# Two small tiles made larger in a hybrid encoder block, so that the matmul operands after them start elsewhere

## The chip, the cores and the metric

The kernel runs on one core of a Trainium2 chip. The metric is the device time of one execution in microseconds (us). "Engines" are TensorE (PE; its weight loads are shown apart as PEld), VectorE (DVE), ScalarE (ACT), GpSimd (POOL) and SyncE (SP), which here issues the DMAs.

## The reference

One encoder layer on 1024 rows of width 1024, in float32:

```python
n = rms_norm(h, attn_norm_w)
aq, ak, av, rq, rk, rv, rg = split(n @ w_in)          # 1024 x 2816
y_attn = windowed_gqa_sink(rope(rms_norm(aq)), rope(rms_norm(ak)), av, sink)
y_ret  = silu(rg) * rms_norm(bidirectional_retention(rope(rq), rope(rk) / 8, rv, log_fwd, log_bwd))
h = h + concat(y_attn, y_ret) @ w_out                 # 1024 x 1024
m = rms_norm(h, ffn_norm_w)
h = h + (silu(m @ w_gate) * (m @ w_up)) @ w_down      # width 2816
```

## The kernel before

Every large operand is split into two float32r tiles, a high part and the rest (`X_hi`/`X_lo`, `wh`/`wl`), and each product is three matmuls: high by high, high by rest, rest by high (`passes`, line 236; `sip`, line 241). A matmul of 128x128 stationary values by a 512-column moving operand writes one PSUM bank. Each matmul has its own weight load, which TensorE runs beside the matmul before it. In rows of the trace, `out<-moving,stationary` is the order of the names.

The work has three stretches. **The front** (to about 526 us) makes the projections: weights come in as tiles of 512 columns and are the *moving* operand, slices of `X_hi`/`X_lo` are stationary (outputs `a`, `b`, `c`, `d`, `o`; `c` in halves of 256 columns). Between these matmuls stand those of retention and attention, which use tiles of the pool `up`; `fill(n)` puts in 3n projection matmuls at given points of the code. **Gate and up** (to about 961 us; `gate_up`, line 986) goes over 22 units, each with seven products of 12 matmuls (a Strassen-like scheme): four with `X_hi`/`X_lo` as the moving operand (the first into `pa`, one into `pb`, two into `pc`), three with `T2`, `T3`, `T4` (all into `pa`); here the weight tile is stationary. **Down** (to about 1171 us; `down`, line 1056) is seven products of 11 x 12 matmuls (`da`, `db`, `dc`), both operands from the weight tiles (`eA..`, `eS..`, tags `wh` and `wl`).

The order of the instructions is set by priorities in the program, and semaphores by what reads and writes which tile. Where a tile stands in a partition of SBUF is set by the pools: one after the other in the order of the code (`const`, `wp`, then `fc`, `up`, `st` of the front; after the front the pools `p2` and `pd` take their place), each tile rounded up to a multiple of 32 bytes. A partition is a run of bytes, and "place" below is the start of an operand in it, as the rest by division by 128. All slices of a tile that matmuls read lie whole multiples of 128 bytes behind its start.

Of the kernel before, what the change touches and what calls it, by code (L numbers as in the profile page):

```python
# [9 lines left out]
F32 = mybir.dt.float32  # L10
F32R = mybir.dt.float32r
AF = mybir.ActivationFunctionType
# [4 lines left out]
P = 128  # L17
# [43 lines left out]
def hymba_block(ctx, tc, x, xT, cst, prm, retw, ffnw, wqkv, wkv, wout, wg, wu, wd, out):  # L61
# [3 lines left out]
    nc = tc.nc  # L65
# [31 lines left out]
    pe, act, dve, pool = (Engine(e) for e in (nc.tensor, nc.scalar, nc.vector, nc.gpsimd))  # L97
# [24 lines left out]
    const = ctx.enter_context(tc.tile_pool(name="const", bufs=1))  # L122
# [4 lines left out]
    fc = front.enter_context(tc.tile_pool(name="fc", bufs=1))  # L127
# [33 lines left out]
    mask = fc.tile([P, 3 * P], F32, name="mask")  # L161
    idx = const.tile([P, 4], F32, name="idx")
    anw = const.tile([P, 8], F32, name="anw")
    prmt = fc.tile([P, 280], F32, name="prmt")
    retw_dm = const.tile([P, DM], F32, name="retw_dm", tag="c4")
    retw_t = retw_dm[:, 0:512]
    mhalf = const.tile([P, 8], F32, name="mhalf")
# [6 lines left out]
    ze = const.tile([P, 2, 8], F32, name="ze")  # L174
    gall = const.tile([P, 2, 8], F32, name="gall")
    gt = const.tile([P, 2, 4], F32, name="gt")

    X_hi = const.tile([P, 8, S], F32R, name="X_hi")
    X_lo = const.tile([P, 8, S], F32R, name="X_lo")
# [132 lines left out]
    def row_rms(t):  # L312
        i = xcount[0] % 8
        xcount[0] += 2
        xv = xs[:, i:i + 2, :]
        nc.sync.dma_start(xv, x[t * P:(t + 1) * P, :].rearrange("p (a c) -> p a c", a=2))
        c = slice(t, t + 1)
        act.activation(xv, xv, AF.Square, accum_out=ssq[:, c])
        dve.tensor_scalar(ssq[:, c], ssq[:, c], 1.0 / DM, EPS, op0=ALU.mult, op1=ALU.add)
        pool.tensor_tensor(rstd[:, c], ssq[:, c], mhalf[:, 0:1], op=ALU.pow)  # L320
        dve.tensor_scalar(rstd8[:, c], rstd[:, c], HD ** -0.5, None, op0=ALU.mult)
        dve.scalar_tensor_tensor(r2[:, c], rstd[:, c], 1.0 / HD, rstd[:, c], op0=ALU.mult, op1=ALU.mult)

    pool.memset(mhalf[:], -0.5)
    warm = const.tile([P, 1], F32, name="warm")

    hold[0] = pinned[0] = True
    act.activation(warm[:], mhalf[:, 0:1], AF.Exp)

    zero = U("zero", "kr", F32R)  # L330
    pool.memset(f32(zero[:]), 0.0)
# [4 lines left out]
    hold[0] = pinned[0] = False  # L336
    for t in range(RMS_AHEAD):
        row_rms(t)
    nc.sync.dma_start(prmt[:], prm)
    nc.sync.dma_start(idx[:], cst[:, 1792:1796])  # L340
    nc.sync.dma_start(cosT[:].rearrange("p t d -> p (t d)"), cst[:, 0:512])
    nc.sync.dma_start(sinT[:].rearrange("p t d -> p (t d)"), cst[:, 512:1024])
# [831 lines left out]
```

## Time and profile before

| | us |
|---|---|
| median of 3 runs | 1179.77 (1178.02 to 1179.95) |
| the profiled execution | 1178.03, span 1176.3 |
| PE busy | 1139.5 (97%) |
| DVE busy | 834.6 (71%) |
| ACT busy | 547.6 (47%) |

A matmul's duration in the trace (about 0.39 us for 512 columns) contains its way through the array, which overlaps the next matmul. What a matmul costs in a full stream is the distance from its start to the next one's start. The chain of waits gives it directly: a piece of n matmuls and its us.

The matmuls of the program before, by width of the moving operand and by place of both operands:

| moving columns | place of moving | place of stationary | matmuls | which |
|---|---|---|---|---|
| 512 | 32 | 0 | 1344 | projections |
| 512 | 0 | 32 | 1056 | gate and up, with X |
| 512 | 32 | 32 | 792 + 924 | gate and up with T; down |
| 512 | 0 | 0 | 100 | attention, and 12 at the start (`idle`) |
| 256 | 32 | 0 | 192 | projection `c` |
| 256, 384 | 0 | 0 | 416 | retention, attention |
| 128 | 0 | 0 or 32 | 560 | transposes, retention |

### The profile page before, as it was taken

What the parts mean: (1) busy time and instruction counts of PE and PEld (TensorE: products, weight loads), DVE (VectorE), ACT (ScalarE), POOL (GpSimd) and SP (SyncE); (2) the same over time, 40 slices, a digit from 0 to 9 for tenths busy, and PEclk for the clock granted to TensorE, in tenths of its full rate; (3) what the DMA queues carried; (4) which work ended last, traced back from release to release, by engine and by line L of the source; (5) the groups of instructions that cost most, each with busy time, mean ns of one, the idle gap of its engine ahead of it and who ended that gap; (6) DMA issues with size and microseconds to landing.
All of it is one profiled execution on the core that took longest, in us unless ns stands there. A gap on an engine that the chain in (4) does not pass through costs nothing.

```text
span 1176.3 us, 16106 instructions
## 1 busy us (share of the span) xinstructions
PE 1139.5 (97%) x5384; PEld 926.9 (79%) x5384; DVE 834.6 (71%) x1632; ACT 547.6 (47%) x1134; POOL 248.5 (21%) x308
## 2 busy tenths in 40 slices
PE   8989998998999999999999999999999999999998
PEld 6767776787878887877888888888888888888887
DVE  6988876888889993689766676567657755555553
ACT  4745534445488863456333333333333335444441
POOL 3445734367545631322000000000000000000000
PEclk9999999999999999999999999999999999999999
DMA  8520112003100023621643554355435668676672
GB/s 290 194 72 1 39 34 70 3 1 91 37 1 2 18 73 112 210 90 63 198 135 124 179 183 138 118 179 187 143 112 177 216 208 290 215 241 192 217 264 72
DMA packets 82594, 152.59 MB, mean 130 GB/s; under 512 B 9424, under 2 KB 9936, under 8 KB 82512
## 3 DMA queue, kind: packets, MB, share of 16 engines
q1 hardware_dynamic: 82512, 151.57, 39.7%
q8 instruction: 42, 0.69, 0.3%
q14 instruction: 40, 0.33, 0.1%
HBM read 111.43 MB, written 40.11 MB: 129 GB/s over the span
## 4 chain that ended last, share of the span: by engine, by line
PE 54%; DVE 3%; issue 2%; POOL 0%; ACT 0%; ACTq 0%; DVEq 0%; POOLq 0%
PE pa L88 21%; PE pc L88 11%; PE da L88 10%; PE dc L88 5%; PE pb L88 5%; PE db L88 3%; DVE h L88 1%; DVE X_lo L88 0%; DVE T L88 0%; DVE xr L88 0%; POOL hr L88 0%; DVE t L88 0%; DVE stash L88 0%; DVE hr L88 0%; DVE S_00l L88 0%
## 5 line engine op out<-in xcount | busy, mean ns | idle before, releaser
L91 POOL TENSOR_TENSOR wl<-raw,wh 128x512 fp32r<-128x512 f32 x44 | 60.2, 1391 | 61.5 <-ACT wh L91 61.0
L88 PE MATMUL a<-wh,X_lo 128*128 128x512 f32 x128 | 51.8, 405 | 1.5 <-DVE X_lo L88 1.4
L88 PE MATMUL a<-wh,X_hi 128*128 128x512 f32 x128 | 51.2, 400 | 1.4 <-DVE krv L88 1.4
L88 PE MATMUL b<-wh,X_hi 128*128 128x512 f32 x128 | 52.4, 409 | 0.0
L88 PE MATMUL o<-wh,X_hi 128*128 128x512 f32 x128 | 51.8, 405 | 0.0
L88 PE MATMUL b<-wh,X_lo 128*128 128x512 f32 x128 | 51.8, 404 | 0.0
L88 PE MATMUL a<-wl,X_hi 128*128 128x512 f32 x128 | 51.3, 401 | 0.0
L88 PE MATMUL b<-wl,X_hi 128*128 128x512 f32 x128 | 51.1, 399 | 0.0
L88 PE MATMUL o<-wh,X_lo 128*128 128x512 f32 x128 | 50.9, 397 | 0.0
L88 PE MATMUL o<-wl,X_hi 128*128 128x512 f32 x128 | 50.9, 397 | 0.0
L88 DVE TENSOR_TENSOR S<-A,A 128x512 f32<-128x512 f32 x44 | 31.3, 711 | 1.6 <-DMA A<-in_wg_dram 1.1
L88 PEld LDWEIGHTS a<-wh,X_lo 128*128 128x128 f32 x128 | 24.4, 190 | 9.0 <-DVE X_lo L88 4.0
L91 ACT CAST wh<-raw 128x512 fp32r<-128x512 f32 x44 | 25.7, 616 | 9.5 <-PE o L88 4.8
L88 PEld LDWEIGHTS a<-wh,X_hi 128*128 128x128 f32 x128 | 24.2, 189 | 6.7 <-issue 2.3
L88 PEld LDWEIGHTS b<-wh,X_lo 128*128 128x128 f32 x128 | 24.4, 190 | 5.2
L88 PEld LDWEIGHTS o<-wh,X_lo 128*128 128x128 f32 x128 | 24.1, 188 | 5.3
L88 ACT ACTIVATE sg<-sg 128x512 f32<-128x512 f32 x33 | 20.9, 632 | 15.8 <-DVE sg L88 15.8
L88 PEld LDWEIGHTS a<-wl,X_hi 128*128 128x128 f32 x128 | 24.4, 190 | 4.7 <-POOL wl L88 0.2
L88 PEld LDWEIGHTS o<-wh,X_hi 128*128 128x128 f32 x128 | 24.1, 188 | 5.0
L88 PEld LDWEIGHTS b<-wl,X_hi 128*128 128x128 f32 x128 | 24.5, 191 | 4.4
L88 PEld LDWEIGHTS o<-wl,X_hi 128*128 128x128 f32 x128 | 24.1, 189 | 4.8
L88 PEld LDWEIGHTS b<-wh,X_hi 128*128 128x128 f32 x128 | 24.6, 192 | 3.8
(2950 smaller groups left out, 3798.6 us busy)
## 6 DMA issues: line engine op xcount, KB each, us to landing
A<-in_wg_dram SPq DMA_DIRECT2D x44, 256.0 KB, 2.8
A<-in_wu_dram SPq DMA_DIRECT2D x44, 256.0 KB, 3.0
R<-in_wd_dram SPq DMA_DIRECT2D x44, 256.0 KB, 2.7
L_S<-LS SPq DMA_DIRECT2D x44, 256.0 KB, 2.3
R_T<-RT SPq DMA_DIRECT2D x44, 256.0 KB, 2.1
raw<-in_wqkv_dram SPq DMA_DIRECT2D x40, 256.0 KB, 2.9
L_A<-a SPq DMA_DIRECT2D x33, 256.0 KB, 2.3
xs<-in_xT_dram SPq DMA_DIRECT2D x16, 256.0 KB, 5.5
```

What stands on the lines that cost most here:

```text
L88: ins = fn(*args, **kw)
L91: ins = fn(*args, **kw)
```

## The change

The tile `warm` (one value per partition, never read) gets 32 columns, of which the first is written as before. The tile `prmt` gets 288 columns, of which the first 280 are used as before. Nothing else is changed; every engine has the same instructions in the same order.

```diff
-    prmt = fc.tile([P, 280], F32, name="prmt")
+    prmt_ = fc.tile([P, 288], F32, name="prmt")
+    prmt = prmt_[:, :280]
...
-    warm = const.tile([P, 1], F32, name="warm")
+    warm = const.tile([P, 32], F32, name="warm")
...
-    act.activation(warm[:], mhalf[:, 0:1], AF.Exp)
+    act.activation(warm[:, 0:1], mhalf[:, 0:1], AF.Exp)
...
-    nc.sync.dma_start(prmt[:], prm)
+    nc.sync.dma_start(prmt, prm)
```

`warm` takes 128 bytes in place of 32, so all that follows moves by 96; `prmt` takes 1152 in place of 1120, so what follows it in the front moves by 128. Starts in bytes:

| tile | before | place | after | place |
|---|---|---|---|---|
| X_hi, X_lo | 6272, 39040 | 0 | the same | 0 |
| first weight tile of tag wh, of wl | 86304, 106784 | 32 | 86400, 106880 | 0 |
| T2 (T3, T4 like it) | 127264 | 32 | 127360 | 0 |
| tiles of `up` (BD) | 135040 | 0 | 135168 | 0 |

After the change all 5384 matmuls have both operands at place 0.

## Rows read from the trace of the kernel before

**Rows 1.** The page: busy time, share of the span, instructions; then the granted clock.
```profile
span 1176.3 us, 16106 instructions
PE 1139.5 (97%) x5384; PEld 926.9 (79%) x5384; DVE 834.6 (71%) x1632; ACT 547.6 (47%) x1134; POOL 248.5 (21%) x308
...
PEclk9999999999999999999999999999999999999999
```
**Rows 2.** Busy time by stretch: us, PE, PEld, DVE, ACT, POOL, clock, DMA.
```profile
0.00:526.00 526.00, 496.19 (x2596) 403.58 (x2596) 424.86 (x995) 290.46 (x692) 242.15 (x303) 0.99 0.23 75
526.00:961.00 435.00, 431.85 (x1857) 348.55 (x1858) 295.06 (x459) 167.38 (x287) 6.34 (x5) 1.00 0.47 153
961.00:1171.00 210.00, 210.00 (x928) 173.91 (x927) 112.56 (x177) 89.73 (x157) 0.00 (x0) 1.00 0.67 217
```
**Rows 3.** Chain of waits, one gate-and-up unit: start us, us, what.
```profile
594.92 2.80 PE pb L88 x12
597.72 2.76 PE pa L88 x12
600.48 2.81 PE pc L88 x12
603.29 2.76 PE pa L88 x12
606.05 2.81 PE pc L88 x12
608.87 5.57 PE pa L88 x24
```
**Rows 4.** Chain of waits, down.
```profile
962.98 29.92 PE da L88 x132
...
1112.58 29.92 PE dc L88 x132
```
**Rows 5.** Matmuls in time, projection `o` (22 starts apart): start us, us, engine, operation.
```profile
508.64 0.40 PE L88 MATMUL o<-wl,X_hi 128*128 128x512 f32 x1
...
513.80 0.39 PE L88 MATMUL o<-wh,X_lo 128*128 128x512 f32 x1
```
**Rows 6.** Matmuls in time, one T product from its first to the next product's first.
```profile
700.73 0.63 PE L88 MATMUL pa<-T,S_40h 128*128 128x512 f32 x2
...
702.81 0.62 PE L88 MATMUL pa<-T,S_40h 128*128 128x512 f32 x2
703.26 0.39 PE L88 MATMUL pa<-T,S_40l 128*128 128x512 f32 x1
703.49 0.40 PE L88 MATMUL pc<-X_hi,S_40h 128*128 128x512 f32 x1
```
**Rows 7.** Matmuls in time: the twelve idle ones at the start, then their last three.
```profile
1.34 4.57 PE L88 MATMUL idle<-zero 128*128 128x512 f32 x12 [1.34 <-POOL zero L88]
...
5.04 0.86 PE L88 MATMUL idle<-zero 128*128 128x512 f32 x3
5.74 0.46 PE L88 MATMUL a<-wh,X_hi 128*128 128x512 f32 x1
```
**Rows 8.** Matmuls in time, retention's 256 columns (10 starts apart).
```profile
128.56 0.28 PE L88 MATMUL r05s<-BD,r05qkl 128*128 128x256 f32 x1
...
129.76 0.39 PE L88 MATMUL b<-wh,X_hi 128*128 128x512 f32 x1
```
**Rows 9.** Matmuls in time, projection `c` in 256 columns (12 starts apart).
```profile
284.48 0.28 PE L88 MATMUL c<-wh,X_hi 128*128 128x256 f32 x1
...
285.89 0.28 PE L88 MATMUL c<-wh,X_hi 128*128 128x256 f32 x1
```
**Rows 10.** Groups of weight loads: busy us, mean ns.
```profile
L88 PEld LDWEIGHTS o<-wh,X_hi 128*128 128x128 f32 x128 | 24.1, 188 | 5.0
L88 PEld LDWEIGHTS pa<-T,S_10h 128*128 128x128 f32 x16 | 3.0, 188 | 0.7
```
**Rows 11.** What PE waited for: us in total, times, longest.
```profile
PE a06pk L88 <- DVE a06vl L88: 3.2, 1, 3.2
PE r16pt L88 <- DVE r16qr L88: 2.0, 1, 2.0
```

## Prediction

> **What bounds the kernel now.** I read the page first: PE is busy for 97% of the span and its clock is full nearly throughout [rows 1]. Then the busy time by stretch: behind the front, PE has no gap at all in down and 3 us of gaps in gate and up, while in the front it stands idle for 526 − 496 = 30 us [rows 2]. From 526 us on, then, the end is set by how far apart the matmuls start; no transfer and no other engine has a say. So the chain of waits is the view that counts, because it gives that distance without the overlap that a matmul's own duration contains. It shows something that the instructions do not explain. All these matmuls have 512 moving columns, a weight load each and the same clock, yet they do not cost the same:
>
> - down: 29.92 us for 132, that is 226.7 ns each, in six pieces out of six [rows 4]; both operands at place 32;
> - gate and up with X: 2.80 or 2.81 for 12, 233.3 to 234.2 ns [rows 3]; moving at 0, stationary at 32;
> - gate and up with T: 2.76 for 12, 230 ns [rows 3]; both at 32;
> - projection: 22 starts in 5.16 us, 234.5 ns [rows 5]; moving at 32, stationary at 0.
>
> The clean division is by whether the two operands stand at the same place. The T products look like an exception, but are not. Their first nine matmuls, which follow an X product, take 702.81 − 700.73 = 2.08 us, 231 ns each, and the last three 703.49 − 702.81 = 0.68 us, 226.7 ns, exactly the figure of down [rows 6]. So a stream whose operands stand alike runs in at 226.7 ns after about nine matmuls, and one whose operands stand differently stays at 233 to 234.5. The weight load itself is as long from either place, 188 ns [rows 10]; it is the load and the matmul beside each other that cost more or less.
>
> The change puts every operand at place 0. What the trace cannot show is whether two operands at 0 meet as well as two at 32.
>
> **The change part by part.** No instruction is added, removed or moved, and no wait. The larger `warm` and `prmt` cost no time of their own: the same elements are written by the same instructions. What is left is the price of 4216 matmuls of 512 columns.
>
> Gate and up, X products: 22 units times four products. A unit's four are 2.80 + 2.81 + 2.81 and the first of the next, 5.57 − 2.76 = 2.81, together 11.23 us [rows 3]. At 226.7 ns twelve take 2.72, four 10.88. Saved 0.35 per unit, **7.7 us**. All of it is on the path, because PE has no gaps there.
>
> Gate and up, T products: 3 × (2.76 − 2.72) × 22 = **2.6 us**, because nothing in the stretch differs any more and the run-in disappears.
>
> Down: 226.7 already, **0**, if place 0 is as good as place 32.
>
> Projections: 1344 matmuls at 234.5 − 226.7 = 7.8 ns are 10.5 us at most [rows 5]. Two things take from it. Projection matmuls are put between other work in lots of 6 to 21 (`fill` of 2 to 7), and a stream takes some nine matmuls to settle [rows 6], so perhaps half are settled. And PE already waits 30 us in the front, the largest pieces for DVE chains that follow a projection tile (3.2 us, 2.0 us) [rows 2, 11]; a faster PE arrives earlier at those. DVE is busy 425 of these 526 us, so where it is late, the time comes back as a longer wait. The bounds are 0 and 10.5; I take 40%, **4.2 us**.
>
> Projection `c` has 256 columns: 12 in 1.41 us, 117.5 ns, with the places different [rows 9]; retention with both at 0 has 10 in 1.20 us, 120 ns [rows 8]. So 192 matmuls may get 2.5 ns dearer, **0.5 us** lost, partly under waits; I leave it within the rounding.
>
> The sum is 7.7 + 2.6 + 4.2 = 14.5 us. From the profiled execution's 1178.0 that gives 1163.5; the median of the runs shown is 1.7 higher, so the forecast is **1165 us**. Its own range is 1159 (all of the 10.5 kept) to 1169.5 (none).
>
> What price two operands at place 0 really have in 512 columns is the unknown, and the trace bounds it from both sides. For 226.7 speaks that retention's matmuls, all at place 0, settle at one figure, 120 ns, which is 13.3 over the 256/2.4 = 106.7 ns of their columns; down's 226.7 is 13.3 over its 512/2.4 = 213.3 as well [rows 4, 8]. The same surcharge at both places is what I would expect if only the difference counts. Against it stand the last idle matmuls: three in 5.74 − 5.04 = 0.70 us, 233 ns, with both operands at place 0, although the nine before them took (5.04 − 1.34) / 9 = 411 ns each, so that these came right behind a change of pace [rows 7]. The upper bound is the projection's 234.5. I take 226.7 as the nearer in kind.
>
> **The rivals.**
>
> *The place within 128 bytes is not the cause (no change).* X is in all of the slow streams, and it is also the one large operand far below the others in memory; the trace cannot separate "X stands elsewhere in the line" from "X is X". Then X stays slow, T runs in again after each X product, and down is as it was: 1179.8, give or take 1. A variant with the same time is that the operands must agree over a longer stretch than 128 bytes: after the change X stands at 128 and the weights at 384 of 512 bytes, so they would still differ, while T and the weights still agree. For it: only two places occur before. Against it: projections have the roles exchanged and are as slow, and retention at place 0 shows the even 120 ns. This is also what the Trainium skill would say: its page "SBUF — State Buffer" (Specifications, and Who interferes with whom) gives SBUF lines of 16 bytes and TensorE two independent read ports, one for the moving operand and one for weight loads. By that rule places 0 and 32 are the same thing and the load costs the matmul nothing; the difference between [rows 3] and [rows 4] does not agree with that, since something beside the column count differs there.
>
> *Place 32 is the good one (slower).* If the absolute place decides and two operands at 0 cost what the mixed ones do, 233.5 ns, then down loses 924 × 6.8 ns = 6.3 us and the T products 792 × 3.5 = 2.8, and the X products and projections stay: 1188.9. It decides as soon as place 0 costs more than about 231 ns: there, down's loss of 924 × 4.3 = 4.0 us and the T products' 0.8 just meet the gain of X (1056 × 2.9 = 3.1) and of the kept projections (1344 × 3.5 × 0.4 = 1.9). For it: the idle matmuls [rows 7]. Against it: the unsettled start of those, and retention.
>
> *The gain is there, but the front keeps none of it, or the match is only partial*: between 1167 and 1177, as faster.
>
> **How the numbers follow.** The forecast with its partial variants has 0.63. No change, by either of the two ways or by a place-0 price near 231, has 0.21. Slower has 0.16. A difference under 0.2% (2.4 us) can't be told from none. The range reaches from 1158, a little under the forecast's own lower end, over the no-change case to 1181; what is left out is most of the slower case and a price below 226.7, for which no row speaks.
>
> **What would show it.** In the chain of waits after, a gate-and-up product of 12 should be 2.72 for X and T alike, and down's pieces of 132 still 29.92. If X products stay at 2.81, the first rival holds; if down's pieces rise towards 30.8, the second. In the front, the starts of `o` should come down to about 227 ns where they run long, and PE's idle 30 us should grow by about half of what its busy time loses. The forecast is wrong if gate and up does not shrink from 435 us to about 425.

## The result and the profile after

The changed kernel takes 1167.24 us (median of 4, 1166.34 to 1168.37) against 1178.89 for the one before (median of 4, 1177.85 to 1179.95): ratio 0.9902, interval 0.9884 to 0.9919. It is faster by 11.65 us; 14.5 were forecast.

The page after: span; busy time, share, instructions; granted clock.

```profile
span 1165.6 us, 16106 instructions
PE 1128.6 (97%) x5384; PEld 928.2 (80%) x5384; DVE 833.0 (71%) x1632; ACT 548.2 (47%) x1134; POOL 248.2 (21%) x308
...
PEclk9989999999999999999999999999999999999999
```

With [rows 1]: the span is 10.7 us shorter and PE's busy time 10.9, while PEld, DVE, ACT and POOL keep theirs within 1.6. So the same matmuls stand closer together.

The chain of waits after, one gate-and-up unit and the first two pieces of down (start us, us, what):

```profile
593.26 2.72 PE pb L88 x12
595.98 2.72 PE pa L88 x12
598.70 2.72 PE pc L88 x12
601.42 2.72 PE pa L88 x12
604.14 2.72 PE pc L88 x12
...
952.30 29.97 PE da L88 x132
982.27 29.92 PE db L88 x132
```

Against [rows 3], X and T products alike come to 2.72, which is 226.7 ns each; against [rows 4], down stays. Where the 10.7 us of span came from is read at two borders. The first gate-and-up matmul, before and then after:

```profile
527.43 0.47 PE L88 MATMUL pa<-X_hi,A_00h 128*128 128x512 f32 x1
```

```profile
526.36 0.47 PE L88 MATMUL pa<-X_hi,A_00h 128*128 128x512 f32 x1
```

The front gave 1.07 us. Gate and up went from 962.98 − 527.43 = 435.55 to 952.30 − 526.36 = 425.94, 9.61 less. From there to the end it is 1176.3 − 962.98 = 213.3 before and 1165.6 − 952.30 = 213.3 after: nothing. The three add up to the span.

In the front the matmuls did become cheaper. Projection `o`, 22 starts apart, after (22 in 5.16 us in [rows 5]):

```profile
506.73 0.39 PE L88 MATMUL o<-wl,X_hi 128*128 128x512 f32 x1
...
511.76 0.39 PE L88 MATMUL o<-wh,X_lo 128*128 128x512 f32 x1
```

That is 5.03 us or 228.6 ns, and the front's gain is small beside it. So for the most part the front's chain must run elsewhere. In retention, one step of it after:

```profile
110.77 1.02 POOL r02rn L88
...
113.33 0.48 DVE r04qr L88
113.81 0.72 DVE r03sl L88
...
115.26 0.57 POOL BD L88
...
116.58 0.76 POOL vhl L88
117.33 2.07 issue
...
119.44 1.02 POOL r03rn L88
```

A step is 119.44 − 110.77 = 8.67 us, and no matmul is in it (in the piece `issue` POOL waits for `r03ss` of DVE). The chain before does not reach back this far, but POOL's own rows of before show the same step:

```profile
111.05 1.01 POOL L88 TENSOR_TENSOR r02rn<-r02ss,mhalf 128x4 f32<-128x4 f32 x1 [2.10 <-DVE r02ss L88]
...
119.72 1.01 POOL L88 TENSOR_TENSOR r03rn<-r03ss,mhalf 128x4 f32<-128x4 f32 x1 [2.11 <-DVE r03ss L88]
```

That is 8.67 us as well: dear or cheap projections beside it make no difference to a step of retention. At the tail of the front the chain looks like this before:

```profile
505.40 4.43 issue
509.86 0.56 POOL hr L88
...
512.56 1.29 DVE t L88 x2
```

And like this after:

```profile
504.33 4.42 issue
508.79 0.56 POOL hr L88
...
511.49 1.28 DVE t L88 x2
```

It is the same chain, 1.07 us earlier and not shorter, though the 22 matmuls of `o` beside it are 0.13 us shorter. Between the end of attention and this tail, PE is the chain after:

```profile
450.12 28.39 PE o L88 x125
```

That is 227.1 ns a matmul, so a long run of projections comes down nearly to 226.7; the 228.6 above contain the run-in. There the front gained most of what it kept. The first of the last three attention outputs, before and then after, is only 0.37 us earlier:

```profile
449.42 0.39 PE L91 MATMUL q71o<-q71pl,V 128*128 128x512 f32 x1
```

```profile
449.05 0.39 PE L91 MATMUL q71o<-q71pl,V 128*128 128x512 f32 x1
```

### The profile page after: what moved, and what is told of

Read it like the earlier page. It is cut to its first block, busy times and chain, and to the rows that moved or that the text cites. A ratio compares the mean times of both kernels' runs of the same rounds, so it can differ in the third digit from the quotient of the medians.

```text
span 1165.6 us, 16106 instructions
## 1 busy us (share of the span) xinstructions
PE 1128.6 (97%) x5384; PEld 928.2 (80%) x5384; DVE 833.0 (71%) x1632; ACT 548.2 (47%) x1134; POOL 248.2 (21%) x308
## 4 chain that ended last, share of the span: by engine, by line
PE 70%; DVE 16%; issue 5%; POOL 5%; DMA 3%; ACT 1%; SPq 0%; POOLq 0%; DVEq 0%; ACTq 0%
PE pa L88 20%; PE da L88 10%; PE pc L88 10%; PE dc L88 5%; PE pb L88 5%; PE a L88 4%; PE o L88 4%; PE db L88 3%; PE d L88 3%; PE c L88 1%; DVE X_lo L88 1%; PE b L88 1%; POOL Y L88 1%; DMA xs<-in_xT_dram 1%; DVE h L88 1%
```

## The experiments

The theory T: a stream of matmuls costs 226.7 ns per 512 columns where moving and stationary operand begin at the same place, and 230 to 235 where they don't. Rivals: X is slow as such; only place 0, or only 32, is good; the stretch over which they must agree is shorter or longer than 128 bytes. "Difference" below is the start of the weight tiles minus that of X, modulo 256: 160 before, 0 after.

**All at place 32** (from the kernel before)

```diff
-    gt = const.tile([P, 2, 4], F32, name="gt")
+    gt_ = const.tile([P, 16], F32, name="gt")
+    gt = gt_[:, :8].rearrange("p (f j) -> p f j", f=2)
-    warm = const.tile([P, 1], F32, name="warm")
+    warm = const.tile([P, 32], F32, name="warm")
```

> From the kernel before; X_hi and X_lo are moved by 32 bytes (the tile gt in front of them takes 64 bytes instead of 32) and the weight tiles and T by 128, so that X, weights and T all stand at place 32. Theory (only the difference between the places of the moving operand and of the stationary operand counts, modulo 128): as the changed kernel, a gate-and-up product 2.72 us for X and T alike, time about 1167 us, ratio 0.990. Rival (X is slow unless the weights are at the start of a 128-byte line, or X is slow unless it is itself there): X products stay at 2.80 us or above, time about 1179 us, ratio 1.000.

Measured: 1167.39 us (1167.25 to 1167.72), ratio 0.9905 [0.989, 0.992]. Its chain:

```profile
593.23 2.72 PE pb L88 x12
595.95 2.72 PE pa L88 x12
```

The place itself doesn't matter and X isn't slow as such; with places 0 and 32, it is agreement that counts.

**Difference 64, and difference 96** (from the kernel before; modulo 256 they are 192 and 224)

```diff
-    warm = const.tile([P, 1], F32, name="warm")
+    warm = const.tile([P, 16], F32, name="warm")   # 24 in the second
```

> From the kernel before; warm takes 64 bytes, so weights and T stand at place 64 and X at 0. Theory (modulo 128): X products and projections stay slow, 231 to 236 ns a matmul, down 226.7 ns, time 1176 to 1182 us. Rival (the stretch that counts is 64 bytes): 226.7 ns everywhere, time about 1167 us, ratio 0.990.

> From the kernel before; warm takes 96 bytes, so weights and T stand at place 96 and X at 0. Theory (modulo 128, moving minus stationary): the difference of 96 is the one of -32, so projections and X products exchange their prices of before: X products about 2.81 us for 12 (234.3 ns, the projections' figure), projections about 233.3 ns; down 226.7 ns; time 1177 to 1182 us. Rival (the price grows with the distance): X products above 236 ns a matmul, 2.84 us, time above 1182 us.

Measured: 1175.18 (1173.56 to 1175.74), ratio 0.9963 [0.9947, 0.9978], and 1178.23 (1176.05 to 1179.25), ratio 0.9987 [0.9978, 0.9996]. The chain at 64:

```profile
595.80 2.75 PE pb L88 x12
598.55 2.77 PE pa L88 x12
```

And at 96:

```profile
596.51 2.80 PE pb L88 x12
599.31 2.76 PE pa L88 x12
```

At 96 X products are as slow as before. At 64 they lie between (2.75, or 229 ns; the theory had asked for 231 to 236, and the time is also a little below its 1176), while T, whose operands agree, is no better than before (2.77): a product takes some of its pace from its neighbours. That 64 would do is excluded. That X and the projections would exchange their prices at 96 did not come: both stood near 233.

**warm alone** (`prmt` as before)

```diff
-    warm = const.tile([P, 1], F32, name="warm")
+    warm = const.tile([P, 32], F32, name="warm")
```

> One half of the change: warm takes 128 bytes, prmt stays. X, weights and T at place 0, the front's small tiles (pool up) at place 96. Theory: the small tiles meet only each other in large matmuls, so their place does not count; as the changed kernel, 1167 us, ratio 0.990. Rival (the front's tiles have to be at place 0 too): the matmuls of retention and attention become dearer and the front grows, 1169 us or more.

Measured: 1166.51 (1165.73 to 1168.13), ratio 0.9899 [0.9884, 0.9914], as with both edits. The half of the change that moves the small tiles of the front does nothing that can be measured.

**Difference 128** (from the kernel before; X, weights and T at place 0, as after the change, but weights and T 128 bytes further on)

```diff
-    warm = const.tile([P, 1], F32, name="warm")
+    warm = const.tile([P, 64], F32, name="warm")
```

> From the kernel before; warm takes 256 bytes, so that weights and T stand at place 0 as in the changed kernel, but 128 bytes further: X and the weights, which agreed modulo 256 there, now differ by 128 modulo 256. Theory (the stretch is 128 bytes): X products 2.72 us, 1166 to 1168. Rival (256 bytes): X products and projections slow again, 1174 to 1181.

Measured: 1175.93 (1174.66 to 1177.29), ratio 0.9975 [0.9966, 0.9984].

```profile
596.29 2.80 PE pb L88 x12
599.09 2.73 PE pa L88 x12
601.82 2.79 PE pc L88 x12
```

X products are slow again, though X and the weights stand at the same place of a 128-byte line. So the theory held with the wrong stretch: they must agree modulo 256. In the changed kernel X (6272) and the weights (86400) both stand at 128 modulo 256; modulo 512 they differ by 256 and are fast all the same. That 128 sufficed was luck of these sizes. Taken as moving minus stationary, X products and projections of the four kernels that differ cover all seven other multiples of 32 within 256; the 2.75 for 12 above is the nearest to 2.72.

**Rest tiles apart** (from the kernel after; 32 bytes between the tiles `wh` and `wl`, so that the rest tiles and T stand at 32, X and `wh` at 0)

```diff
+        if i == 0:
+            wp.tile([P, 8], F32, name="apart", tag="apart", bufs=1)
```

> The changed kernel with 32 bytes between the weight tiles of the high parts (place 0) and those of the rests (place 32, and T with them). Theory (a matmul meets the weight load of the NEXT matmul, which runs beside it): in down the moving operand and the next load agree in all three passes (0 and 0, 32 and 32, 0 and 0), so 29.92 us for 132 as before, although one matmul in three streams from another place than its own weights had; X products have one disagreeing pair in three, T products two, so they lie between 2.72 and 2.81; time 1170 to 1176. Rival (a matmul's own two operands have to agree): down has two disagreeing in three and takes more than 30.3 us for 132.

Measured: 1183.0 (1182.66 to 1184.08), ratio 1.004 [1.0025, 1.0055], slower than the kernel before.

```profile
594.89 2.80 PE pb L88 x12
597.69 2.79 PE pa L88 x12
600.48 2.77 PE pc L88 x12
...
962.61 30.64 PE da L88 x132
```

Down rises from 226.7 to 232.2 ns, so the theory that a matmul meets the load of the next one only fails, and its time of 1170 to 1176 with it. If the matmul's own operands decided alone, one in three in down agreed and two differed, at (3 × 232.2 − 226.7) / 2 = 235 ns, near [rows 5]; but by the same count X products, two thirds of which agree, should take about 2.75 and take 2.77 to 2.80. Whether the own operands count or the whole stream stays open, and with it the prediction's sentence that the load and the matmul beside each other cost more.

**Where the front's share went: idle PE filled with repeats.** In the profile after, the granted clock is at half in more places of the front (below). Did that eat the gain? In both kernels matmuls are repeated at three waits (22, 13 and 13 times, with the same result, so work is added and none left out), which keeps PE busy there.

```diff
+SPIN = (("a06pk", 0, 22), ("r06pt", 1, 13), ("r16pt", 1, 13))
...
+    for ahead, of, n in SPIN:   # repeat matmul `of` of this tile n times, ahead of the next one
```

> The changed kernel with the same order on every engine; ahead of three matmuls that wait in the front (a06pk's second, 3.2 us; r06pt's and r16pt's third, 1.9 us each) the matmul before them in the same PSUM tile is repeated 22, 13 and 13 times with the same result, so that PE is busy while it waits. In the profile of the changed kernel the granted clock falls to half for 3.4 or 6.8 us right behind those waits, in the kernel before only behind one of them. Theory C (the falls ate the front's gain): with fewer falls the front is 4 to 5 us shorter, time about 1162.5. Theory D (the front's end is set by chains over DVE and POOL and neither PE's rate nor its clock counts there): the falls go, the time stays, 1166 to 1168.5.

> The kernel before with the same repeats. Theory C: one fall less, about 1.6 us shorter, 1178. Theory D: 1178 to 1181 and the same front as the other one up to the end of attention.

Measured: 1165.37 (1165.07 to 1165.66), ratio 0.9889 [0.9874, 0.9904], and 1177.35 (1176.67 to 1178.86), ratio 0.9991 [0.9981, 1.0]. The first gate-and-up matmul of the repeated kernel before, and of the repeated one after:

```profile
525.99 0.47 PE L91 MATMUL pa<-X_hi,A_00h 128*128 128x512 f32 x1
```

```profile
525.03 0.48 PE L91 MATMUL pa<-X_hi,A_00h 128*128 128x512 f32 x1
```

Their fronts differ by 0.96 us, as without repeats (1.07), although the clock falls only once in the front of the one and twice in that of the other. The 4 to 5 us of theory C are not there. Theory D is not exact either: both medians lie 0.6 us below its ranges. The repeated kernel after is the fastest measured, but its interval overlaps that of the change alone.

**More work in the front** (from the kernel after; the transposes of all 16 `r..pt` of retention repeated 8 times, 14.0 us more work on PE, none left out)

```diff
+SPIN = tuple((f"r{g}{c}pt", 1, 8) for g in range(2) for c in range(8))
```

> The changed kernel with the same order; in each of the 16 retention steps of the front the transpose ahead of the two that wait for the query rows is repeated 8 times with the same result: 128 more instructions of 109 ns, 14.0 us more work for PE, where the front's gain was at most 10.5 us. Theory D (PE is off the path in retention): 1165 to 1170. Rival (PE is on the path there and the gain was lost otherwise): up to 14 us longer, 1178 to 1181.

Measured: 1173.2 (1172.79 to 1174.21), ratio 0.9952 [0.9937, 0.9967].

```profile
532.80 0.47 PE L91 MATMUL pa<-X_hi,A_00h 128*128 128x512 f32 x1
```

The front grew by 532.80 − 526.36 = 6.4 us of 14.0, between the two theories, so it settles less than hoped. A step of retention, 8.67 in both kernels, is 9.33 here (`r02rn` starts at 112.49, `r03rn` at 121.82). Of the 8 × 109 ns = 0.87 us added to a step, 0.66 come back: the repeats stand at transposes whose results DVE reads, not in the projections beside the chain. So these transposes have little slack, while cheaper projections change nothing in a step. PE is only partly on the front's path.

**The front's small tiles agree modulo 256 as well** (from the kernel after; the second run with the three repeats too)

```diff
-    prmt_ = fc.tile([P, 288], F32, name="prmt")
+    prmt_ = fc.tile([P, 320], F32, name="prmt")
```

> The changed kernel with prmt of 1280 bytes instead of 1152, so that the front's tiles of pool up, which stood at 0 modulo 256 while X and the weights stand at 128, now stand at 128 too: every operand of every large matmul agrees modulo 256. Theory (agreement modulo 256, and a stream needs matmuls to settle after work at another place): the projections, which lie between retention and attention, come down from 228 to 230 ns towards 227; but the front is not set by PE, so 1165.5 to 1167.5. Rival (the front pays for it): 1163 to 1165.

> e10 with the repeats of e5, the candidate for the fastest. Theory: as e5, 1164 to 1166, ratio 0.988 to 0.989. Rival (both add up with a gain of the front's own): 1161 to 1163.5.

Measured: 1166.87 (1166.51 to 1167.62), ratio 0.9898 [0.9883, 0.9913], and 1166.21 (1165.54 to 1166.97), ratio 0.989 [0.9873, 0.9906]. No effect of the tiles on the time: runs of 22 projections stay at 227 to 228.5 ns, so what holds them above 226.7 is not the place of the tiles between them.

## Why the prediction was right, and the term that was off

- *The cause.* Right: agreement of the two places sets the distance of matmuls; X, weights and T at 32 give the same time as every operand at 0. That the change brought them together modulo 256 too was luck, for places were counted modulo 128. The variant of the first rival that asked for a longer stretch than 128 bytes had the better rule (256, not 512); it gave "no change" only by its wrong length.
- *Price at place 0.* Taken as 226.7 of bounds up to 234.5; down and gate and up after show 226.7. The idle matmuls [rows 7] were no guide, as argued.
- *X and T products, 10.3 us.* Gate and up shrank by 9.61. Each product has the forecast 2.72. Of the missing 0.7, 0.4 is waiting: PE is idle for 435.55 − 432.79 = 2.76 us of the stretch before and 425.94 − 422.79 = 3.15 after, and after there is a wait at its start that before doesn't have (us in total, times, longest):

```profile
PE pa L88 <- DVE T L88: 1.3, 1, 1.3
```

  It needs no cheaper matmuls, for the repeated kernel before has it too (1.4). What the rest is stays open. In the six other profiled runs with X, weights and T in agreement the stretch takes 425.3 to 425.5, that is 10.0 to 10.3 less than 435.55. The repeated pair, whose down begins at 961.59 before and 950.30 after, goes from 435.60 to 425.27, by 10.3 as forecast.
- *Down, 0.* Right.
- *Projections, 4.2 us.* This term was too large: 1.07 in the profiled pair. Their price fell further than assumed (from 234.5 to 227.1 in the long run, where half was taken as settled); the share of it that shortens the run was set too high. The 40% came from PE's 30 idle us of 526, read as a stretch that PE nearly bounds. A step of retention takes 8.67 us with either price, and the tail's chain is the same in both kernels: both run over DVE and POOL. Of the front's whole chain after, projections hold 27% (`a` 8.1, `o` 7.9, `d` 5.6, `c` 2.9, `b` 2.6). The sign named for this, PE's idle time growing by half of what its busy time loses, does not show in the profiled pair. Its fronts (us, PE busy, ...), before and then after:

```profile
0.00:527.43 527.43, 497.23 (x2604) 404.41 (x2605) 426.29 (x998) 291.89 (x695) 242.15 (x303) 0.99 0.23 75
```

```profile
0.00:526.36 526.36, 496.33 (x2605) 406.32 (x2605) 424.98 (x998) 292.62 (x695) 241.87 (x303) 0.98 0.24 75
```

  Busy time lost 0.9 and idle time stayed at 30.2 and 30.0, for after stands at half clock for longer, where matmuls take more time. In the repeated pair busy goes from 501.08 to 498.69 and idle from 24.9 to 26.3: 1.4 of 2.4 come back as waiting.

  How little was kept depends on the pair. In the three other runs with agreement and no added work (all at 32, `warm` alone, the front's small tiles) the medians are 12.1 to 13.3 below that of the kernel before run beside them; less the 10.0 to 10.3 of gate and up, the front kept about 2 to 3 there, near 27% of 10.5. 1.07 is the low end.
- *`c`.* 12 of 256 columns took 1.44 us after (284.84 to 286.28), 120 ns against 117.5 in [rows 9]: the small loss came as estimated.

Of the 14.5 the profiled pair shows 10.7: 3.1 are missing in the front, 0.7 in gate and up. The medians differ by 11.65, since the profiled execution of before was one of its quicker ones, with a mean granted clock of 0.995; others of the same kernel had 0.989 to 0.996.

The Trainium skill says otherwise on the cause: its page "SBUF — State Buffer" (SBUF: two separate sides) has PE never waiting on anyone, with a second, independent read port for weight loads. Independence of PE's own two reads does not agree with the runs here, as far as the distance of matmuls goes: with the same instructions and the same loads of 188 ns, a product of 12 takes 2.72, 2.75 or 2.80 by the difference of two addresses. The measurement decides. Which part of the chip the two reads meet in, no run shows.

## What to carry to other kernels

Where PE has no gaps, compare the distance of starts between streams of the same shape; a few ns that differ by which tile is moving and which stationary can be an address, and a pad of 96 bytes was worth 1%. Here the moving and the stationary operand wanted to agree modulo 256 bytes, and with high and rest tiles 32 bytes apart the kernel was slower than before. A saving on an engine that is 94% busy in a stretch is not 94% kept: follow the chain there before a share is put on it, and take its size from more than one execution.

## What the runs showed of the hardware

**256 columns go the other way**: 120 ns where the places agree and 117.5 where they don't, by the two stretches of `c` above, while 512 columns gain 7.8. The runs don't explain it.

**The best stream is still above its columns.** 226.7 ns is 13.3 over 512/2.4 = 213.3. The Trainium skill's page "TensorE: Matmul & The Clock Gate" (Wait — 56ns, not 53.3ns?) gives about 2.5 over the columns, 215.7 measured. These streams, float32r with a load for each matmul, don't reach that in any run here; what the rest is stays open.

**A halved clock that costs little.** Busy time by stretch before (us, PE, PEld, DVE, ACT, POOL, granted clock, DMA share, GB/s):

```profile
131.60:135.00 3.40, 1.71 (x12) 1.22 (x11) 3.34 (x5) 1.92 (x4) 3.27 (x5) 1.00 0.07 22
135.00:138.40 3.40, 3.13 (x15) 2.59 (x16) 3.14 (x7) 2.55 (x6) 1.59 (x3) 1.00 0.40 135
```

And after:

```profile
131.60:135.00 3.40, 1.48 (x12) 1.06 (x10) 3.34 (x6) 1.62 (x4) 3.39 (x4) 1.00 0.11 27
135.00:138.40 3.40, 3.40 (x9) 2.74 (x10) 2.90 (x6) 2.65 (x7) 1.49 (x3) 0.50 0.44 130
```

After, PE is a little more idle ahead of 135 us (1.48 us busy, not 1.71), and behind that the clock is granted at 1.2 GHz, half, for 3.4 us. Such falls stand at three places before and at five after. That cheaper matmuls brought them is not shown: with difference 128, where X products are dear, the clock falls there too, and with all at place 32 it does not. The first of these, then the second:

```profile
136.00:139.30 3.30, 3.30 (x10) 2.56 (x9) 2.45 (x6) 3.13 (x7) 1.49 (x3) 0.50 0.32 85
```

```profile
135.00:138.40 3.40, 2.46 (x12) 2.08 (x13) 3.35 (x5) 1.89 (x5) 2.17 (x3) 1.00 0.50 154
```

With repeats, one is left before and two after, and the medians are 1.5 and 1.9 lower: an estimate of 0.6 to 0.7 per fall if the one profiled execution of each kernel is typical, near what these runs can tell apart at all. At half clock for 3.4 us, PE loses the work of 1.7. So a fall may cost less than it takes from PE, but not because PE was off the path: behind 135 us the chain after runs over PE's slow matmuls (from 135 to 138.4 us).

```profile
135.63 2.95 PE b L88 x7
```

What wins the time back later, the runs don't show.
